# Index stage of a decoder layer: where the last query block's scratch lies and when scratch slots come back

## The chip, the cores and the metric

The kernel runs on one NeuronCore of a Trainium2 chip. The metric is the device time of one execution in microseconds (us). The engines have queues of their own, and each works through its queue in order: TensorE (PE, matmuls and transposes), VectorE (DVE), ScalarE (ACT), GpSimd (POOL, which also issues DMAs) and SyncE (SP, which issues most DMAs). [...]

## What is computed

The reference is one layer of a decoder: two attention mixers side by side (A: sparse attention with an indexer that selects keys; B: latent attention), gates, an output projection and a convolutional feed-forward part, on 512 tokens of width 2048, all in float32. The change lies in mixer A's indexer and in the projection behind it:

```python
dots = jnp.einsum('bthd,bsd->bths', qi_b, ki, preferred_element_type=jnp.float32)
score = jnp.einsum('bths,bth->bts', jax.nn.relu(dots), wi_b.astype(jnp.float32))
score = jnp.where(causal[None], score, -jnp.inf)
_, sel = lax.top_k(score, n_sel)
...
qa = apply_rope(rms_norm(qa.reshape(B, S, A_HEADS, A_HEAD_DIM), g_qa), *rope_a)
```

Each block of 128 queries has 16 index heads of width 64, and n_sel is 128. The first block needs no selection, since it sees at most 128 keys; blocks 1, 2 and 3 see 256, 384 and 512.

## The kernel before

**Buffers.** Storage that moves from use to use is a pool of slots of 128 x 512 numbers. `get()` takes a slot from the head of a list of free ones and `put()` gives one back to its end. Five wide buffers (`quad`, 128 x 2048) first form a ring `aring` through which the columns of w_ada pass; when that stage ends, four of them are taken out of the ring and cut into slots (`quad_views`), and the fifth, `aring[0]`, stays as a ring of one, for the rest of the w_ada stream that runs beside the attention stages. A framework puts a semaphore wait before every instruction that writes a slot which an earlier user still reads.

**Order.** The Python code issues instructions as a program would, and a scheduler then sets the order in each engine's queue by priorities and by a model of time. Which slot a step takes is settled in the Python order; when it may be written is then a matter of the chip.

**Weights.** Products run in three passes on a float32 that is split in a high and a low part. `wtile` loads a weight tile on SP, copies its high part on ACT (L145) and forms the low part on DVE (L146). The three matmuls of a product (`mm3`) stand on L157, L158 and L159. There are five raw buffers and three buffers of split tiles.

**Index stage.** The loop over query blocks `tb` 1 to 3 (L541) rotates the index queries of a block (`rope`, L505 to L508), transposes them (L549), splits them (L153, L154), and then, for each of 16 heads, multiplies with all keys up to S = 256, 384 or 512 (a dot of three matmuls), takes the relu on ACT (L563) into one of three slots `rl`, and adds it, weighted, to `acc` on DVE (L565, L567). The selection is DVE's alone: 16 maxima of eight (L575) with 15 replacements between them (L577) in `wk`, which is `rl[0]`, and then nine short steps (L582 to L591, the scan on L587 among them) that make the block's mask. At its end the four slots `acc`, `rl` are given back, in the Python order before the next block takes its own.

**First projections behind it.** `ev_qa` empties a bank of the query projection of mixer A: it takes a slot, copies the bank (L630), sums squares (L603, L604), normalises and rotates, transposes (L641) and writes the transposed rows (L643). The projection runs twice (`cb` 0 and 1), each time over eight weight tiles into banks 72 to 75 (`MM`), one for each block of tokens. Behind it come a product 320 wide (L793 to L803 empty and use it), one 512 wide, and the attention, whose first step that reads a mask is L684.

**Gate tiles.** Three tiles of the branch gates, computed with the first products into `part["B"][4:7]`, are stored to memory by POOL (L763), in the Python order only just ahead of the attention.

Of the kernel before, what the change touches and what calls it, by code (L numbers as in the profile page):

```python
# [10 lines left out]
F32 = mybir.dt.float32  # L11
# [7 lines left out]
P = 128  # L19
T = 512  # L20
D = 2048
KD = D // P
# [9 lines left out]
def trunk_layer_kernel(  # L32
# [19 lines left out]
    V, A, G, PE, SP = nc.vector, nc.scalar, nc.gpsimd, nc.tensor, nc.sync  # L52
# [4 lines left out]
    dram = ctx.enter_context(tc.tile_pool(name="scratch", bufs=1, space=bass.MemoryType.DRAM))  # L57
# [7 lines left out]
    def get(dt=F32, low=0):  # L65
        i = next((i for i in free if i >= low and (i < n_slots or dt == F32)), None)
        assert i is not None, (dt, list(free))
        free.remove(i)
        if i < n_slots and (cur[i] is None or cur[i].dtype != dt):
            cur[i] = pool.tile([P, T], dt, name=f"slot{i}", tag=f"slot{i}")  # L70
        held[id(cur[i])] = i
        return cur[i]
# [23 lines left out]
    def put(*ts):  # L96
        for t in ts:
            i = held.pop(id(t))
            if not isinstance(i, int):
                rfree.append(i)  # L100
            elif i not in retired:
                free.append(i)
# [53 lines left out]
    def mm3(o, lh, ll, rh, rl, first, last):  # L156
        PE.matmul(o, lh, rh, start=first, stop=False)  # L157
        PE.matmul(o, lh, rl, start=False, stop=False)  # L158
        PE.matmul(o, ll, rh, start=False, stop=last)  # L159
# [20 lines left out]
    def lin_tm(src, c0, n, act, K, banks, evac, k0=0, tick=None):  # L180
        for kg in range(0, K, 2):
            wh, wl = wtile(src, k0 + kg, 2, c0, n)
            for tb in range(4):
                ts = slice(tb * P, (tb + 1) * P)
                for i in range(2):
                    k = kg + i
                    ah, al = act[k]
                    mm3(banks[tb][:, :n], ah[:, ts], al[:, ts], wh[:, i, :], wl[:, i, :],
                        k == 0, k == K - 1)
                if kg + 2 == K:  # L190
                    evac(tb, banks[tb][:, :n])
            if tick:
                tick()
# [22 lines left out]
    aring = deque(quads[1:])  # L216
# [114 lines left out]
    part = {"A": [get() for _ in range(7)], "B": [get() for _ in range(7)]}  # L331
# [111 lines left out]
    f = 0  # L443
# [69 lines left out]
    def at_bank():  # L513
        cnt["at"] += 1
        return AT[cnt["at"] % 4]


    kit = part["A"][6]
    kw_tm = tslot[3][:, 0:320].rearrange("p (t n) -> p t n", t=4)
    kdup = tslot[4].rearrange("p (t a d) -> p t a d", t=4, a=2)  # L520
# [20 lines left out]
    for tb in range(1, 4):  # L541
        S = (tb + 1) * P
        qiT = []
        for cb in range(2):
            t = qi[tb, cb]
            rope(t.rearrange("p (h d) -> p h d", d=64), 8, 16, "i", tb)
            b = at_bank()
            for q in range(4):
                PE.transpose(b[:, q * P:(q + 1) * P], t[:, q * P:(q + 1) * P], ident)  # L549
            o = (getr(), getr())  # L550
            split(*o, b)
            put(t)
            qiT.append(o)
        acc = get()
        rl = [get(), get(), get()]
        for hd in range(16):
            ps = slice((hd % 2) * 64, (hd % 2) * 64 + 64)
            q = (hd % 8) // 2
            b = at_bank()
            (qh, ql), qs = qiT[hd // 8], slice(q * P, (q + 1) * P)  # L560
            mm3(b[:, :S], qh[ps, qs], ql[ps, qs], kiT[0][ps, :S], kiT[1][ps, :S], True, True)
            r = rl[hd % 3]
            A.activation(r[:, :S], b[:, :S], AF.Relu)  # L563
            if hd == 0:
                V.tensor_scalar(acc[:, :S], r[:, :S], wi[:, tb, 0:1], None, op0=ALU.mult)  # L565
            else:
                V.scalar_tensor_tensor(acc[:, :S], r[:, :S], wi[:, tb, hd:hd + 1], acc[:, :S],  # L567
                                       op0=ALU.mult, op1=ALU.add)
        put(*qiT[0], *qiT[1])
        V.tensor_tensor(acc[:, tb * P:S], acc[:, tb * P:S], Z[:, 384:512], ALU.add)  # L570
        m8 = sm.tile([P, 8], F32, name="m8")
        wk = rl[0]
        src = acc
        for it in range(16):
            V.max(m8, src[:, :S])  # L575
            if it < 15:
                V.match_replace(wk[:, :S], m8, src[:, :S], -3e38)  # L577
                src = wk
        thr = m8[:, 7:8]
        gt, eq, pre = rl[1][:, :S], rl[2][:, :S], wk[:, :S]  # L580
        cgt = sm.tile([P, 1], F32, name="cgt")
        V.tensor_scalar(gt, acc[:, :S], thr, None, op0=ALU.is_gt)  # L582
        V.tensor_reduce(cgt, gt, axis=AX.X, op=ALU.add)
        V.tensor_scalar(cgt, cgt, -1.0, 128.0, op0=ALU.mult, op1=ALU.add)
        V.tensor_scalar(eq, acc[:, :S], thr, None, op0=ALU.is_equal)
        V.memset(acc[:, :S], 1.0)
        V.tensor_tensor_scan(pre, acc[:, :S], eq, 0.0, ALU.mult, ALU.add)  # L587
        V.scalar_tensor_tensor(pre, pre, cgt, eq, op0=ALU.is_le, op1=ALU.mult)
        V.tensor_tensor(gt, gt, pre, ALU.add)
        mk = mask_at[tb].bitcast(BF)  # L590
        V.tensor_scalar(mk, gt, -NEG, NEG, op0=ALU.mult, op1=ALU.add)  # L591
        mask[tb] = mk
        put(acc, *rl)
    put(*kiT, tslot[3], tslot[4])
    mask[0] = Z[:, 384:512]

# [30 lines left out]
    def ev_qa(cb):  # L627
        def ev(tb, b):
            t = get()
            A.activation(t, b, AF.Copy)  # L630
            q3 = t.rearrange("p (n d) -> p n d", n=4)
            ss = sm.tile([P, 4], F32, name="ss4")
            head_ss(ss, q3, tb)
            n = nsc_a[:, tb, cb * 4:cb * 4 + 4]
            r = sm.tile([P, 4], F32, name="rs4")
            rsqrt_mean(r, ss, P, 4)
            V.tensor_scalar(n, r, -(P ** -0.5), None, op0=ALU.mult)
            rope(q3, 4, 32, "qa", tb)
            bb = at_bank()
            for q in range(4):  # L640
                PE.transpose(bb[:, q * P:(q + 1) * P], t[:, q * P:(q + 1) * P], ident)  # L641
            o = get()
            A.activation(o, bb, AF.Copy, scale=gq_col)  # L643
            put(t)
            qaT[tb, cb] = o
        return ev

    for cb in range(2):
        lin_tm(w_in, C_QA + cb * 512, 512, h, KD, MM, ev_qa(cb))


    att = {}
# [104 lines left out]
            pairs.append((th, tl))  # L757
        return pairs


    gate_d = [dram.tile([P, T], F32, name=f"gate{k}") for k in range(2 * KD)]
    for m in range(3):
        G.dma_start(gate_d[m], part["B"][4 + m])  # L763
        put(part["B"][4 + m])

    def ev_store(dst, j0):
        def ev(m, b):
# [259 lines left out]
    for i in range(KH // 2):  # L1027
        raw = [get() for _ in range(4)]
        ta, tb_ = get(), get()
        for j in range(2):  # L1030
            k, o = 2 * i + j, slice(j * HT, (j + 1) * HT)
# [692 lines left out]
    for q in range(NS):  # L1724
        p, k = q // NK, q % NK
# [89 lines left out]
```

## Time and profile before

| | |
|---|---|
| median of 3 runs | 2665.16 us (2662.46 to 2666.19) |
| the profiled execution | 2671.87 us |
| its span, first to last instruction | 2670.1 us |
| mean granted TensorE clock | 0.983 |
| index stage, second projection included | about 200 to 352 us of the span |

A row of the timeline reads: start in us, duration in us, engine, line, operation, written<-read, shape, count, and in brackets how long the engine was idle before it and what ended that. A row of the waits reads: who waited, for whom, us in total, times, longest. A row of a group reads: line, engine, operation, shapes, count | busy us, mean ns of one | idle us before it and what ended it. In the names of the trace the numbers are left out: `slot` is a single slot and `quad` a slot cut from a wide buffer.

### The profile page before, as it was taken

How to read it: one execution, taken by the hardware profiler on the slowest of the kernel's cores; microseconds unless marked ns; L12 is line 12 of the kernel's file. 1: busy time of each engine (PE TensorE's matmuls, PEld its weight loads, DVE VectorE, ACT ScalarE, POOL GpSimd, SP SyncE). 2: the span in 40 equal slices, each digit the busy share in tenths (PEclk: the TensorE clock that was granted, in tenths of full speed). 3: DMA queues.
4: the chain of work that ended last, by engine and by line, in shares of the span. 5: the costliest groups of instructions: out<-in, count | busy, mean ns of one | idle time of the engine just before them, and what ended most of it. 6: DMA issues, size and time to landing. Idle time of an engine off the chain costs nothing.

```text
span 2670.1 us, 39567 instructions
## 1 busy us (share of the span) xinstructions
PE 2576.3 (96%) x15210; PEld 2234.5 (84%) x15210; DVE 2109.8 (79%) x3130; ACT 1197.9 (45%) x1714; POOL 247.4 (9%) x483
## 2 busy tenths in 40 slices
PE   7999699998999999999999999999999999999988
PEld 5877487778997767888789999999999987877777
DVE  7968945768888666855679998998998987788876
ACT  5333333334445466322445555555555554443342
POOL 1000010000023132100000000000000000000000
PEclk8999799999999999999999999999999999999999
DMA  9932046663685488876224334434334357797776
GB/s 376 361 129 91 16 125 207 204 199 133 205 265 183 131 261 282 299 241 227 91 80 137 134 127 139 129 116 144 121 129 143 129 182 266 264 342 261 260 265 233
DMA packets 183044, 509.07 MB, mean 191 GB/s; under 512 B 20923, under 2 KB 29557, under 8 KB 182853
## 3 DMA queue, kind: packets, MB, share of 16 engines
q1 hardware_dynamic: 151460, 423.31, 47.2%
q0 software_dynamic: 31360, 83.21, 8.8%
q8 instruction: 119, 1.95, 0.3%
q14 instruction: 73, 0.59, 0.1%
q10 hardware_dynamic: 32, 0.01, 0.0%
HBM read 450.59 MB, written 55.85 MB: 190 GB/s over the span
## 4 chain that ended last, share of the span: by engine, by line
PE 81%; DVE 9%; DMA 7%; issue 1%; ACT 1%; SPq 0%; POOL 0%; DVEq 0%; ACTq 0%
PE bank L157 14%; PE bank L158 14%; PE bank L159 14%; PE bank L1015 11%; PE bank L1014 11%; PE bank L1016 11%; DMA wraw<-in_w_down 4%; DVE wsp L1462 2%; PE bank L703 1%; PE bank L1152 1%; PE bank L695 1%; PE bank L852 1%; DMA quad<-in_w_ada 1%; DVE wraw L1449 1%; DMA slot<-r 1%
## 5 line engine op out<-in xcount | busy, mean ns | idle before, releaser
L1015 PE MATMUL bank<-slot,wsp 128*128 128x256 f32 x2128 | 598.6, 281 | 0.4 <-DVE slot L154 0.4
L1014 PE MATMUL bank<-slot,wsp 128*128 128x256 f32 x2040 | 574.2, 281 | 3.7 <-ACT slot L153 2.5
L1016 PE MATMUL bank<-slot,wsp 128*128 128x256 f32 x2040 | 573.0, 281 | 0.0
L153 ACT ACTIVATE wsp<-wraw 128x1024 fp32r<-128x1024 f32 x336 | 356.5, 1061 | 449.4 <-PE bank L1015 340.6
L154 DVE TENSOR_TENSOR wsp<-wraw,wsp 128x1024 fp32r<-128x1024 f32 x336 | 410.2, 1222 | 76.8 <-ACT wsp L153 75.7
L158 PE MATMUL bank<-wsp,slot 128*128 128x512 f32 (+2 forms) x1108 | 437.0, 395 | 19.4 <-DVE wsp L1462 19.3
L159 PE MATMUL bank<-wsp,slot 128*128 128x512 f32 (+2 forms) x1166 | 450.2, 392 | 0.0
L157 PE MATMUL bank<-wsp,slot 128*128 128x512 f32 (+2 forms) x1108 | 394.3, 392 | 10.4 <-ACT wsp L1460 6.2
L1015 PEld LDWEIGHTS bank<-slot,wsp 128*128 128x128 f32 x2128 | 402.3, 189 | 0.7 <-DVE slot L154 0.6
L1014 PEld LDWEIGHTS bank<-slot,wsp 128*128 128x128 f32 x2040 | 385.7, 189 | 4.4 <-ACT slot L153 3.0
L1016 PEld LDWEIGHTS bank<-slot,wsp 128*128 128x128 f32 x2040 | 385.1, 189 | 0.0
L145 ACT ACTIVATE wsp<-wraw 128x1024 fp32r<-128x1024 f32 (+4 forms) x182 | 187.6, 1032 | 390.5 <-PE bank L159 190.8
L146 DVE TENSOR_TENSOR wsp<-wraw,wsp 128x1024 fp32r<-128x1024 f32 (+4 forms) x182 | 215.9, 1188 | 169.7 <-ACT wsp L145 169.2
L158 PEld LDWEIGHTS bank<-wsp,slot 128*128 128x128 f32 x1108 | 211.5, 191 | 71.2 <-DVE wsp L1462 25.4
L325 DVE CUSTOM_DVE_ANT_0 quad<-quad,quad,col 128x2048 f32<-128x2048 f32 x96 | 225.0, 2347 | 57.9 <-DMA quad<-in_w_ada 57.9
L159 PEld LDWEIGHTS bank<-wsp,slot 128*128 128x128 f32 x1166 | 222.4, 191 | 47.8 <-DVE slot L411 0.7
L157 PEld LDWEIGHTS bank<-wsp,slot 128*128 128x128 f32 x1108 | 209.9, 190 | 58.5 <-ACT wsp L1460 6.9
L907 DVE TENSOR_TENSOR wraw<-wraw 128x1024 f32<-128x1024 f32 x192 | 233.9, 1218 | 3.8 <-DMA wraw<-in_w_gs 2.0
L1460 ACT ACTIVATE wsp<-wraw 128x1536 fp32r<-128x1536 f32 (+1 forms) x109 | 151.5, 1397 | 154.1 <-DVE wraw L1452 80.7
L1462 DVE TENSOR_TENSOR wsp<-wraw,wsp 128x1536 fp32r<-128x1536 f32 (+1 forms) x109 | 179.0, 1645 | 29.2 <-ACT wsp L1460 29.2
L158 PE MATMUL bank<-slot,wsp 128*128 128x512 f32 (+1 forms) x414 | 166.2, 402 | 0.0
L157 PE MATMUL bank<-slot,wsp 128*128 128x512 f32 (+1 forms) x389 | 156.0, 405 | 0.0
(574 smaller groups left out, 4389.3 us busy)
## 6 DMA issues: line engine op xcount, KB each, us to landing
quad<-in_w_ada SPq DMA_DIRECT2D x192, 512.0 KB, 5.6
wraw<-in_w_ups SPq DMA_DIRECT2D x160, 512.0 KB, 3.4
wraw<-in_w_down SPq DMA_DIRECT2D x87, 768.0 KB, 5.8
wraw<-in_w_in SPq DMA_DIRECT2D x50, 512.0 KB, 3.5
wraw<-in_w_gs SPq DMA_DIRECT2D x32, 512.0 KB, 4.5
wraw<-in_w_o SPq DMA_DIRECT2D x32, 512.0 KB, 5.4
quad<-in_w_down SPq DMA_DIRECT2D x47, 256.0 KB, 4.5
wraw<-in_w_down SPq DMA_DIRECT2D x44, 256.0 KB, 5.4
```

The source lines that it names most:

```text
L146: w_ins[1] = V.tensor_tensor(lo, raw[:, :w], r32(hi), ALU.subtract)
L153: A.activation(dst_hi, src, AF.Copy)
L154: return V.tensor_tensor(dst_lo, src, r32(dst_hi), ALU.subtract)
L157: PE.matmul(o, lh, rh, start=first, stop=False)
L158: PE.matmul(o, lh, rl, start=False, stop=False)
L159: PE.matmul(o, ll, rh, start=False, stop=last)
L325: V.tensor_tensor_reduce(t, t, crow, 1.0, col1[:, j:j + 1], ALU.mult, ALU.add, mod[:, j:j + 1])
L907: V.tensor_tensor(o[:, :WN], a[:, :WN], b[:, :WN], op)
L1014: PE.matmul(o, wh[:, ks], rh, start=first and k == 0, stop=False, skip_group_check=True)
L1015: PE.matmul(o, wh[:, ks], rl, start=False, stop=False, skip_group_check=True)
L1016: PE.matmul(o, wl[:, ks], rh, start=False, stop=last, skip_group_check=True)
L1462: r = V.tensor_tensor(lo, t, r32(hi), ALU.subtract)
```

## The change

It does three things. The scratch of the third block that is worked on (`tb` 3) is no longer four slots but the four quarters of `aring[0]`. The scratch of `tb` 2 is kept in a list `busy` and given back only when both query projections have been issued; only that of `tb` 1 is given back in the loop. And the code that stores the three gate tiles, which gives their three slots back, moves ahead of the index stage.

```diff
+    gate_d = [dram.tile([P, T], F32, name=f"gate{k}") for k in range(2 * KD)]
+    for m in range(3):
+        G.dma_start(gate_d[m], part["B"][4 + m])
+        put(part["B"][4 + m])
+
     kit = part["A"][6]
...
-        acc = get()
-        rl = [get(), get(), get()]
+        if tb < 3:
+            acc, *rl = (get() for _ in range(4))
+        else:
+            acc, *rl = (aring[0][:, o:o + T] for o in range(0, 4 * T, T))
         for hd in range(16):
...
         mask[tb] = mk
-        put(acc, *rl)
+        if tb == 1:
+            put(acc, *rl)
+        elif tb == 2:
+            busy = [acc, *rl]
     put(*kiT, tslot[3], tslot[4])
...
     for cb in range(2):
         lin_tm(w_in, C_QA + cb * 512, 512, h, KD, MM, ev_qa(cb))
+    put(*busy)
...
-
-    gate_d = [dram.tile([P, T], F32, name=f"gate{k}") for k in range(2 * KD)]
-    for m in range(3):
-        G.dma_start(gate_d[m], part["B"][4 + m])
-        put(part["B"][4 + m])
```

The slots that later steps get change with it, and the scheduler orders the index stage and the projections anew. Line numbers behind the first insertion grow by 5, then by 7 and 10: L563, L567, L575, L577, L603, L630 and L641 of before are L570, L574, L582, L584, L613, L640 and L651 of the change.

On ACT, where the first query projection is emptied, before (`quad_70` is scratch of block 2, `slot_321` and `quad_71` of block 1, `slot_294` to `slot_298` of block 3; banks 72 to 75 hold the projection):

```order
L563 ACTIVATE slot_298<-bank_79 128x512
L630 ACTIVATE slot_321<-bank_72 128x512
L603 ACTIVATE slot_132<-slot_321 128x512
L563 ACTIVATE slot_294<-bank_76 128x512
L563 ACTIVATE slot_296<-bank_77 128x512
L603 ACTIVATE slot_132<-slot_325 128x512
L563 ACTIVATE slot_298<-bank_78 128x512
L630 ACTIVATE quad_71<-bank_73 128x512
```

And the last of the four, some ten rows further on in the same queue:

```order
L643 ACTIVATE slot_326<-bank_79,col_135 128x512
L643 ACTIVATE quad_71<-bank_78,col_135 128x512
L630 ACTIVATE quad_70<-bank_75 128x512
L603 ACTIVATE slot_329<-quad_70 128x512
L145 ACTIVATE wsp<-wraw 128x1024 x3
```

ACT's queue with the change, the same four steps (the relus around them are now those of block 2, 384 wide):

```order
L640 ACTIVATE slot_132<-bank_72 128x512
L613 ACTIVATE slot_133<-slot_132 128x512
L640 ACTIVATE slot_335<-bank_73 128x512
L613 ACTIVATE slot_294<-slot_335 128x512
L640 ACTIVATE slot_329<-bank_74 128x512
L613 ACTIVATE slot_133<-slot_329 128x512
L570 ACTIVATE quad_70<-bank_77 128x384
L570 ACTIVATE quad_70<-bank_78 128x384
L570 ACTIVATE quad_70<-bank_79 128x384
L145 ACTIVATE wsp<-wraw 128x1024
L640 ACTIVATE slot_324<-bank_75 128x512
```

The four copies now stand together, ahead of the dots of block 3, and none of their slots is scratch of a block.

On DVE, the weight splits (L146) around the end of block 2's selection, before (`m_1881` belongs to block 3):

```order
L591 TENSOR_SCALAR slot_316<-quad_70 128x384
L268 TENSOR_SCALAR rsm<-ss_2253 128x4
L577 MATCH_REPLACE slot_294<-m_1881,slot_294 128x512
L146 TENSOR_TENSOR wsp<-wraw,wsp 128x1024
L575 MAX m_1881<-slot_294 128x8
L637 TENSOR_SCALAR nsc_a<-rs_2256 128x4
L577 MATCH_REPLACE slot_294<-m_1881,slot_294 128x512
L146 TENSOR_TENSOR wsp<-wraw,wsp 128x1024
```

DVE with the change, the 15th split of the two projections (`quad_69` is the wide buffer, `quad_70` and `m_1773` belong to block 2):

```order
L574 SCALAR_TENSOR_TENSOR quad_69<-quad_69,wi 128x512
L584 MATCH_REPLACE quad_70<-m_1773,quad_70 128x384
L146 TENSOR_TENSOR wsp<-wraw,wsp 128x1024
L598 TENSOR_SCALAR wraw<-quad_71 128x256
L574 SCALAR_TENSOR_TENSOR quad_69<-quad_69,wi 128x512
L582 MAX m_1773<-quad_70 128x8
```

Before, no split stood between the 11th, early in block 2's sums, and the 12th, which is the first shown here, behind the mask of block 2 (L591). With the change the 11th to the 16th are spread over block 2's sums and selection and block 3's sums.

On PE, the second projection around the dots of block 3. Before, at the place where bank 75 is taken again (`wsp` are weights; `quad_70` is the first projection's fourth copy):

```order
L159 MATMUL bank_75<-wsp,slot_591 128x512
L641 MATMUL bank_76<-ident,quad_70 128x128 x4
L157 MATMUL bank_72<-wsp,slot_657 128x512
L157 MATMUL bank_73<-wsp,slot_657 128x512
L157 MATMUL bank_74<-wsp,slot_657 128x512
L157 MATMUL bank_75<-wsp,slot_657 128x512
```

PE with the change (rows from `quad_1359`, `quad_1360` are dots of block 3):

```order
L157 MATMUL bank_79<-quad_1359,quad_1360 128x512
L158 MATMUL bank_79<-quad_1359,quad_1360 128x512
L159 MATMUL bank_79<-quad_1359,quad_1360 128x512
L157 MATMUL bank_73<-wsp,slot_798 128x512
L158 MATMUL bank_73<-wsp,slot_798 128x512
L159 MATMUL bank_73<-wsp,slot_799 128x512
L157 MATMUL bank_76<-quad_1359,quad_1360 128x512
L158 MATMUL bank_76<-quad_1359,quad_1360 128x512
L159 MATMUL bank_76<-quad_1359,quad_1360 128x512
L157 MATMUL bank_74<-wsp,slot_754 128x512
```

Before, the first three tiles of the second projection ran bank by bank, with bank 75 last and all dots of block 3 ahead of it; now its matmuls and the dots alternate. Ahead of 200 us and from the attention on, all five queues hold the same instructions in the same order as before, but for one matmul that changes places on PE much later.

## The prediction

> **What bounds the kernel now.** I read the page first, for where TensorE (PE) is not busy; then busy time by stretch; then the waits; then the timeline of ACT and PE.
>
> ```profile
> span 2670.1 us, 39567 instructions
> PE   7999699998999999999999999999999999999988
> PEclk8999799999999999999999999999999999999999
> PE 81%; DVE 9%; DMA 7%; issue 1%; ACT 1%; SPq 0%; POOL 0%; DVEq 0%; ACTq 0%
> ```
>
> PE carries the chain that ended last. After the start the only weak slice is the fifth (267 to 334 us), with six tenths of PE and seven of its clock: the index stage. By stretch:
>
> ```profile
> 257.90:272.00 14.10, 13.60 (x73) 9.77 (x73) 13.75 (x38) 7.66 (x15) 0.00 (x0) 1.00 0.12 38
> 272.00:296.30 24.30, 22.53 (x84) 15.28 (x82) 24.30 (x70) 11.96 (x21) 3.46 (x3) 0.79 0.00 0
> 296.30:317.00 20.70, 0.00 (x0) 0.00 (x0) 20.67 (x56) 1.59 (x3) 0.00 (x0) 0.59 0.00 0
> 317.00:351.60 34.60, 34.57 (x145) 28.07 (x146) 27.95 (x64) 11.89 (x16) 2.55 (x3) 0.95 0.24 68
> 351.60:381.20 29.60, 29.60 (x207) 29.57 (x206) 10.88 (x29) 12.42 (x25) 3.48 (x5) 1.00 0.38 118
> ```
>
> The columns are the stretch and its length, then busy us (and instructions) of PE, weight load, DVE, ACT, POOL, then PE's clock and DMA. PE does nothing for 20.7 us from 296.3. DVE is full from 272 to 317, and half empty again from 351.6.
>
> ```profile
> PE bank L157 <- ACT quad L630: 20.7, 1, 20.7
> ACT quad L630 <- DVE quad L587: 19.1, 1, 19.1
> 256.00 0.62 ACT L630 ACTIVATE slot<-bank 128x512 f32<-128x512 f32 x1
> 279.68 0.60 ACT L630 ACTIVATE slot<-bank 128x512 f32<-128x512 f32 x1
> 285.65 0.59 ACT L630 ACTIVATE quad<-bank 128x512 f32<-128x512 f32 x1
> 316.38 0.60 ACT L630 ACTIVATE quad<-bank 128x512 f32<-128x512 f32 x1 [19.09 <-DVE quad L587]
> 317.03 0.80 PE L157 MATMUL bank<-wsp 128*128 128x512 f32 x1 [20.75 <-ACT quad L630]
> ```
>
> L630 empties a bank of the first query projection into a slot. Of its four calls the third has a free slot and runs at 256.00. The first two take scratch of query block 1 and wait for its selection (279.68, 285.65). The last takes `quad_70`, scratch of query block 2, whose selection reads it last in the scan of L587, so it runs at 316.38. Bank 75 stays full until then, and PE's queue has the second projection's matmuls on that bank next. So what ends last is a slot, not arithmetic.
>
> **The change part by part.** No instruction is added or removed on any engine; the order differs only between about 200 and 440 us.
>
> *The stall.* PE's own work in the stretch is counted from its queue, at these paces:
>
> ```profile
> 254.67 0.34 PE L157 MATMUL bank<-quad,quad 64*128 64x384 f32 x1
> 254.85 0.34 PE L158 MATMUL bank<-quad,quad 64*128 64x384 f32 x1
> 257.48 0.39 PE L158 MATMUL bank<-wsp,slot 128*128 128x512 f32 x1
> 257.71 0.40 PE L159 MATMUL bank<-wsp,slot 128*128 128x512 f32 x1
> 273.31 0.49 PE L157 MATMUL bank<-quad,quad 64*128 64x512 f32 x1 [0.55 <-ACT slot L563]
> 282.75 0.63 PE L157 MATMUL bank<-wsp 128*128 128x512 f32 x1
> 283.18 0.63 PE L158 MATMUL bank<-wsp 128*128 128x512 f32 x1
> ```
>
> From start to start a 512-wide matmul takes 0.23 us (257.48 to 257.71; 0.231 over longer runs) and a 384-wide one 0.175; at the lowered clock the 512 takes 0.43. The first projection's last matmul ends at 257.9 and the first 320-wide matmul of the next product starts at 351.6: 93.7 us. Between them stand 192 matmuls of the second projection and 48 dots of query block 3 (240 x 0.231 = 55.4), 24 dots of block 2 (4.2) and 32 transposes at about 0.09 (2.9): **62.5 us of work, 31.2 us lost**. Of the loss 20.7 is the stall, 1.8 the nine matmuls at 0.43 instead of 0.23 just after it, and 8.7 the small waits and lowered clock between 268 and 296, where PE has little but block 3's dots and each waits for ACT and DVE. In the new order these dots stand among the second projection's matmuls.
>
> *What is late next: the splits.* Each 1024-wide weight tile needs one split on DVE (L146). Now six of the sixteen (the 11th to the 16th) stand among the selection steps of blocks 1 and 2 and the sums of block 3. DVE's prices:
>
> ```profile
> L146 DVE TENSOR_TENSOR wsp<-wraw,wsp 128x1024 fp32r<-128x1024 f32 x11 | 13.4, 1215 | 4.5 <-ACT wsp L145 4.5
> L567 DVE SCALAR_TENSOR_TENSOR slot<-slot,wi,slot 128x512 f32<-128x512 f32 x15 | 11.0, 732 | 0.0
> L567 DVE SCALAR_TENSOR_TENSOR quad<-quad,wi 128x384 f32<-128x384 f32 x15 | 9.1, 606 | 0.4 <-ACT quad L563 0.4
> L575 DVE MAX8 m<-quad 128x8 f32<-128x384 f32 x16 | 8.6, 537 | 0.0
> L577 DVE MATCH_REPLACE8 quad<-m,quad 128x384 f32<-128x384 f32 x15 | 8.0, 531 | 0.0
> L575 DVE MAX8 m<-slot 128x8 f32<-128x256 f32 x16 | 6.8, 422 | 0.1
> L577 DVE MATCH_REPLACE8 slot<-m,slot 128x256 f32<-128x256 f32 x15 | 6.1, 409 | 0.0
> L567 DVE SCALAR_TENSOR_TENSOR slot<-quad,wi,slot 128x256 f32<-128x256 f32 x10 | 4.8, 484 | 4.4 <-ACT quad L563 3.9
> L567 DVE SCALAR_TENSOR_TENSOR slot<-slot,wi,slot 128x256 f32<-128x256 f32 x5 | 2.4, 485 | 1.0 <-ACT slot L563 0.7
> 249.86 1.23 DVE L146 TENSOR_TENSOR wsp<-wraw,wsp 128x1024 fp32r<-128x1024 f32 x1 [0.51 <-ACT wsp L145]
> 297.47 0.67 DVE L575 MAX8 m<-slot 128x8 f32<-128x512 f32 x1
> 298.07 0.53 DVE L575 MAX8 m<-quad 128x8 f32<-128x384 f32 x1
> ```
>
> Mean ns of one stands behind the busy time. The tenth split starts at 249.86; with the six short rows after it DVE comes to the first rope of the emptied projection near 254. From there to the 16th split its queue holds 6 splits (7.3), 14 sums of 512 (10.2) and 13 of 384 (7.9), 9 maxima (4.8) and 9 replacements (5.4, with a value load of 0.07) of 384, 11 and 11 of 256 (4.6 and 5.3), and 41 others, 13.2 by the same view: 58.7 us of durations. Neighbours overlap by 0.06 to 0.07 (297.47 + 0.67 against 298.07), 8 us over 134 instructions, so about 50.5. The 16th split is done between 304.5 and 312.7. PE without waits comes to its tile at 257.9 + 62.5 - 5.5 = 314.9. **The splits are in time, by 2 to 10 us.**
>
> The next product (eight narrow tiles, 29.6 us on PE, row 351.60) brings the end of block 2's selection and most of block 3's: 41.0 us of durations, 35 overlapped, to the last narrow split. That is 340 to 354; PE wants it at 257.9 + 62.5 + 29.6 - 3.7 = 346.3. From 6 early to 7.4 late: a loss of 0 to 7.4, taken at 1. Here alone the cover is thin. Small waits (the first dots behind their splits, transposes behind ropes) I put at 2 more.
>
> *The wide buffer.* Sums from wide and from single slots cost the same (484 and 485 ns above), so the move itself costs 0. But `quad_69` is the ring of the w_ada stream. Its first load, and what else rests on the selection:
>
> ```profile
> 391.78 0.97 SPq L320 DMA_DIRECT2D quad<-in_w_ada  x2
> 339.64 0.43 DVE L591 TENSOR_SCALAR slot<-slot 128x512 bf16<-128x512 f32 x1
> 443.52 0.75 DVE L684 CUSTOM_DVE_ANT_0 slot<-bank,slot,nsc_a 128x512 f32<-128x512 f32 x1
> 201.79 0.62 POOL L763 DMA_DIRECT2D gate<-slot  x1 [182.17 <-DVE rsm L268]
> ```
>
> The load would move from 391.8 to about 361. Block 3's mask, done by 340 before, now stands behind the fourth split of the product after the narrow one, also near 360: the load may wait 0 to 2 us, and the weight loads behind it on SP's queue with it. They run ahead into five buffers; I take 0. The mask is first read by L684, at 443.5 - 31 = 412, 50 us later. So deferring block 3 is covered.
>
> *Held slots and gate stores.* The three stores already ran at 201.79 and in the two us after; they keep their place on POOL's queue: 0. One of their slots, the key tile's, one of block 1 and a free one now take the first projection, so all four banks empty by about 259. Block 2's slots come back after both projections, before anyone asks for them.
>
> **Sum:** 31.2 less 3 = 28 us. The profiled execution took 2671.9 (span 2670.1), so 2643.9 of its kind; the three runs have a median of 2665.2, 6.7 lower, and I predict against that: **2637**. Behind 440 us the queues are as before, but for one matmul, and PE sets the pace, so the gain stays.
>
> **Rivals.**
>
> *DVE becomes the bound.* The last narrow split comes 7.4 late, and block 3's dots cost PE the 8.7 us they cost before although other matmuls stand between: 16 us of the 31 go, 2649 (2643 to 2655). For it: DVE is full and in order, and every relu, rope and split must pass it. Against it: the overlapped sum leaves PE 6 to 10 us.
>
> *The wait only moves.* Another bank finds its slot busy, and the change does not do what it says: about 2664. For it: before, two more of the four calls had waited on a selection (279.68, 285.65). Against it: the four new holders are given up before 259, and none is selection scratch.
>
> *Slower.* PE, fed by DVE in small portions, drops to the low clock and stays there. The row at 282.75 shows this clock after waits of 0.55 us (273.31 and its neighbours). Price: 0.43/0.23 puts 0.86 us on each us of work, 54 on all 62.5, less 31.2: 2688. It decides from 36 of the 62.5 us at the low clock; before, some 14 us ran so (clock 0.79 over 24.3 us and 0.95 over 34.6, in the rows by stretch, if the low clock is half). Against it: a late split makes PE wait once and then run on, and the clock was back after 10 us.
> [...]
>
> **How the numbers follow.** Forecast 0.66 (2632 to 2643), DVE bound 0.24, wait only moved 0.06, slower 0.04. What a measurement can tell from no change is 0.2%, 5.3 us: faster 0.90, same 0.06, slower 0.04. The range runs from 2630 (all 31.2, and runs that spread by 2 to 3 us) to 2655, the end of the second case, and leaves out the last two.
>
> **What would show it.** Right: the four evacuations of the first projection run between 252 and 260 with no wait on DVE; no PE gap over 2 us between 258 and 350; the first 320-wide matmul near 321 to 324 instead of 351.6; L684 some 28 us earlier; all later stages shifted by the same amount. If DVE binds, PE or ACT waits for L146, or for the sums at each dot, and the lowered clock shows. If the wait moved, one gap of 10 us or more stands at another evacuation. Wrong altogether would be a shift at 351.6 that is lost again by 600.

## The result

| | before | with the change |
|---|---|---|
| first comparison: median (lowest to highest), four executions each | 2663.81 us (2662.40 to 2666.19) | 2640.76 us (2635.68 to 2642.41) |
| ratio of the times | | 0.9896, 95% interval 0.9877 to 0.9915 |
| second comparison, later, beside the experiments: median | 2670.16 us | 2637.97 us (2635.52 to 2641.73) |
| ratio | | 0.9881, interval 0.9866 to 0.9896 |
| profiled execution (span) | 2671.87 us (2670.1) | 2642.41 us (2640.6) |

The forecast was 2637. The page of the changed kernel, the lines that answer to those shown of before: its span, PE's busy share and granted clock in 40 slices, and the shares of the chain that ended last.

```profile
span 2640.6 us, 39567 instructions
PE   7999999998999999999999999999999999999988
PEclk8999999999999999999999999999999999999999
PE 84%; DMA 7%; DVE 6%; issue 1%; ACT 1%; SPq 0%; DVEq 0%; ACTq 0%
```

The weak fifth slice is gone from both lines, and DVE's share of the chain has fallen. By stretch, after (the stretch and its length, then busy us and instructions of PE, weight load, DVE, ACT and POOL, then PE's clock and DMA):

```profile
258.00:272.00 14.00, 14.00 (x61) 9.52 (x60) 14.00 (x45) 5.83 (x11) 4.86 (x3) 1.00 0.21 62
272.00:300.00 28.00, 28.00 (x119) 17.88 (x117) 26.32 (x64) 11.87 (x19) 0.00 (x0) 1.00 0.13 36
300.00:326.00 26.00, 26.00 (x126) 20.59 (x126) 22.92 (x56) 13.37 (x21) 0.98 (x1) 1.00 0.14 39
326.00:360.00 34.00, 34.00 (x223) 32.93 (x223) 32.33 (x93) 14.06 (x33) 6.08 (x8) 1.00 0.42 134
```

In these stretches PE is busy in every microsecond and its clock is never lowered. DVE was as full before; now PE is full beside it. The timeline of the first projection's four evacuations on ACT, and of PE where the 320-wide product begins, first of the change, then of before:

```profile
251.93 0.59 ACT L640 ACTIVATE slot<-bank 128x512 f32<-128x512 f32 x1
253.10 0.58 ACT L640 ACTIVATE slot<-bank 128x512 f32<-128x512 f32 x1
254.25 0.58 ACT L640 ACTIVATE slot<-bank 128x512 f32<-128x512 f32 x1
257.88 0.58 ACT L640 ACTIVATE slot<-bank 128x512 f32<-128x512 f32 x1
324.50 0.30 PE L157 MATMUL bank<-wsp 128*128 128x320 f32 x1
```

```profile
351.19 0.30 PE L157 MATMUL bank<-wsp 128*128 128x320 f32 x1
```

No evacuation waits for DVE any more: the last runs at 257.88 instead of 316.38. (The start of the 320-wide product in before is 351.19; the prediction had read 351.6 from the edge of a stretch.)

**A common zero.** Executions differ by up to 5 us in the start-up (the row below starts between 189.96 and 194.81 in the profiles of all kernels here), so places in two traces are compared from a row that stands ahead of everything that the change moves: ACT's copy of a 1024-wide weight tile, near 191 us. Of before, and of the change:

```profile
191.17 1.06 ACT L145 ACTIVATE wsp<-wraw 128x1024 fp32r<-128x1024 f32 x1 [3.92 <-PE bank L158]
```

```profile
190.86 1.06 ACT L145 ACTIVATE wsp<-wraw 128x1024 fp32r<-128x1024 f32 x1 [3.92 <-PE bank L158]
```

From there the 320-wide product begins after 160.0 us before and 133.6 after, 26.4 earlier. The large product near 600 us shows what is left of that. Its summary by line gives counts, durations and the first and last start, of before (L1014) and of the change (L1020):

```profile
L1014 PE MATMUL bank<-wsp x184: 276/281/385, 618.2 to 2193.7; 128*128 128x256 f32 x184
```

```profile
L1020 PE MATMUL bank<-wsp x184: 276/281/385, 591.4 to 2165.2; 128*128 128x256 f32 x184
```

It begins 427.0 us behind the common row before and 400.5 after: 26.5. So the gain arises between 258 and 325 us and stays. These two distances carry most of what follows, since they repeat: two profiles of the change gave 133.6 and 400.5 both times, while their spans differ by 5.3 us (2640.6 and 2635.3), all of it behind 2165. The times follow them only to some us: from its first matmul to its last the large product takes 1575.5 to 1581.6 us in the profiles of all kernels here, and what lies behind it 467 to 477.

### The profile page after: what moved, and what is told of

Same layout as the page of the kernel before. It is cut to its first block, busy times and chain, and to the rows that moved or that the text cites. A ratio compares the mean times of both kernels' runs of the same rounds, so it can differ in the third digit from the quotient of the medians.

```text
span 2640.6 us, 39567 instructions
## 1 busy us (share of the span) xinstructions
PE 2570.7 (97%) x15210; PEld 2225.4 (84%) x15210; DVE 2108.6 (80%) x3130; ACT 1198.3 (45%) x1714; POOL 249.7 (9%) x483
## 4 chain that ended last, share of the span: by engine, by line
PE 84%; DMA 7%; DVE 6%; issue 1%; ACT 1%; SPq 0%; DVEq 0%; ACTq 0%
PE bank L157 15%; PE bank L158 15%; PE bank L159 15%; PE bank L1020 11%; PE bank L1021 11%; PE bank L1022 11%; DMA wraw<-in_w_down 3%; DVE wsp L1468 2%; PE bank L714 1%; PE bank L1158 1%; DMA slot<-r 1%; PE bank L706 1%; PE bank L858 1%; DVE wraw L1455 1%; DMA wraw<-in_w_in 1%
## 5 line engine op out<-in xcount | busy, mean ns | idle before, releaser
L1020 PE MATMUL bank<-slot,wsp 128*128 128x256 f32 x2040 | 573.4, 281 | 3.6 <-ACT slot L153 2.4
L1020 PEld LDWEIGHTS bank<-slot,wsp 128*128 128x128 f32 x2040 | 384.3, 188 | 4.3 <-ACT slot L153 2.9
L146 DVE TENSOR_TENSOR wsp<-wraw,wsp 128x1024 fp32r<-128x1024 f32 (+4 forms) x182 | 215.5, 1187 | 141.8 <-ACT wsp L145 140.9
```

Of the source, the lines that this page charges most:

```text
L146: w_ins[1] = V.tensor_tensor(lo, raw[:, :w], r32(hi), ALU.subtract)
L1020: PE.matmul(o, wh[:, ks], rh, start=first and k == 0, stop=False, skip_group_check=True)
```

## The experiments

The theory, **S**: the slot that each of the four evacuations takes sets the time. Before, the last one took scratch of block 2; any change that keeps the four off that scratch removes the stall, and the gain depends on whether some of them still take scratch of block 1. Its rivals: that the parts of the change add up, each with its own share (A), or that DVE is the bound of this stretch (B and D).

All results in one table; the distances are from the common row to the 320-wide product and to the product near 600.

| kernel | median, us | before beside it | ratio, 95% interval | to 320 | to 600 |
|---|---|---|---|---|---|
| before | | | | 160.0 | 427.0 |
| the change | 2640.76; 2637.97 | 2663.81; 2670.16 | 0.9896 (0.9877 to 0.9915); 0.9881 (0.9866 to 0.9896) | 133.6; 133.6 | 400.5; 400.5 |
| gate stores alone | 2654.11 | 2668.24 | 0.9944 (0.9924 to 0.9964) | 139.0 | 405.9 |
| block 2 held alone | 2661.37 | 2668.24 | 0.9982 (0.9968 to 0.9996) | 131.9 | 417.4 |
| wide buffer alone | 2651.42 | 2668.24 | 0.9929 (0.9906 to 0.9953) | 136.9 | 403.9 |
| wide buffer, gate stores | 2644.98 | 2668.24 | 0.9916 (0.9895 to 0.9938) | 133.6 | 404.7 |
| wide buffer, held | 2645.65 | 2670.16 | 0.9908 (0.9894 to 0.9923) | 135.8 | 402.8 |
| gate stores, blocks 2 and 3 held | 2651.68 | 2671.47 | 0.9924 (0.9896 to 0.9952) | 139.0 | 405.9 |
| the change, fourth copy in block 2's slot | 2672.80 | 2670.16 | 1.0014 (1.0004 to 1.0024) | 160.3 | 427.2 |
| the change, 16 steps more on DVE | 2642.56 | 2671.47 | 0.9892 (0.9866 to 0.9918) | 134.8 | 401.7 |
| the change, 48 steps more on DVE | 2644.14 | 2671.47 | 0.9898 (0.9874 to 0.9922) | 132.2 | 404.2 |
| the change, dots of 128 rows | 2641.64; 2640.70 | 2670.16; 2671.47 | 0.9900 (0.9882 to 0.9917); 0.9885 (0.9858 to 0.9912) | 130.6; 130.6 | 397.5; 397.6 |

### The change again

> The whole change again, to narrow its interval and to stand beside the three others on the same chip. 2636 to 2645 us, 20 to 28 us less than the kernel before on this chip; first 320-wide matmul about 27 us earlier than before.

2637.97 us; the 320-wide product 26.4 us earlier from the common row, as in the first profile.

### One slot put back

```diff
-            t = get()
+            t = busy.pop() if (cb, tb) == (0, 3) else get()
```

> The whole change, but the fourth copy of the first query projection is made to take a slot of block 2's scratch again (the held list gives it), as before the change. Wide buffer, early gate stores and the rest stay. Theory S (the slot of that copy is the cause of the 20.7 us stall): PE stalls at bank 75 until block 2's selection has read its scores, 10 us or more in one piece, and the time is 2652 to 2664 us. Rival (the wide buffer and the new order by themselves bring it, and the slot only went along): 2638 to 2645 us, no gap over 2 us.

The timeline of this kernel, ACT's fourth evacuation and PE's next matmul on that bank:

```profile
315.63 0.60 ACT L640 ACTIVATE quad<-bank 128x512 f32<-128x512 f32 x1 [17.02 <-DVE quad L595]
316.28 0.80 PE L157 MATMUL bank<-wsp 128*128 128x512 f32 x1 [18.39 <-ACT quad L640]
```

One slot gives the whole gain back: 18.4 us of stall in one piece, again behind the selection of block 2, and 160.3 and 427.2 us on the table, those of before. The time (2672.80) lies above the range given. The wide buffer, the early stores and three held slots are all still there. The edit is not a pure one: with that slot the scheduler, which models the wait, also puts the fourth evacuation some 30 rows later in ACT's queue, and the rows of PE and DVE around it with it. Slot and order go together here, and the trace shows only that the wait on the selection is what ends last. That the slot is enough without that order is not shown by this kernel; the three below, which take the last copy off block 2's scratch in three other ways, all lose the stall.

### Each part alone

Each is the kernel before with one hunk of the diff. Of gate stores alone:

```diff
+    for m in range(3):
+        G.dma_start(gate_d[m], part["B"][4 + m])
+        put(part["B"][4 + m])
+
     kit = part["A"][6]
```

> The kernel before with the early gate stores alone: the scratch of block 3 is in single slots again and all scratch is given back in the loop, so of the change only the two or three slots that come back earlier are left. The first query projection is then emptied into two free slots and into two slots of block 1's scratch, and none of its four copies takes a slot of block 2. Theory S (what counts is the slot that each of the four copies takes): the stall of 20.7 us at bank 75 goes though neither the wide buffer nor the held slots are there; two copies still wait for block 1's selection, which ends near 280 us, so some of the 8.7 us of small waits stay. Expected 2641 to 2650 us, against 2664 before and 2641 with the whole change. Rival A (the wide buffer and the held slots bring the time, the gate stores only fit in): 2659 to 2664. Rival B (DVE is close to the bound, and only the spread of the splits saved it): the stall turns up at another bank, 2655 to 2664, with PE waiting for L146.

Of block 2 held alone:

```diff
-        put(acc, *rl)
+        if tb == 2:
+            busy = [acc, *rl]
+        else:
+            put(acc, *rl)
...
+    put(*busy)
```

> The kernel before with the held scratch of block 2 alone. Two of the four copies of the first projection take free slots, two take slots of block 1's scratch, none a slot of block 2. Theory S: as with the gate stores alone, 2641 to 2650 us. Rival A1 (the parts add up, and the held slots are the smaller part beside the wide buffer): 2655 to 2664. Rival A2 (the held slots are the change, the two others only keep the pool from running dry): 2641, and the gate stores alone and the wide buffer alone at 2659 or more.

Of the wide buffer alone:

```diff
+        if tb < 3:
+            acc, *rl = (get() for _ in range(4))
+        else:
+            acc, *rl = (aring[0][:, o:o + T] for o in range(0, 4 * T, T))
...
-        put(acc, *rl)
+        if tb < 3:
+            put(acc, *rl)
```

> The kernel before with the wide buffer for block 3 alone. Two of the four copies take free slots, two take slots of block 1's scratch. Theory S: as the two others, 2641 to 2650 us; the sum of the three single gains is then two to three times the gain of the whole change. Rival A (parts add up): the three single gains add to the 23 us of the whole, so this one gives at most what the other two leave.

In all three the four evacuations are over by 294 us and the 20.7 us stall at bank 75 is gone, with 21.0, 28.1 and 23.1 us gained at the 320-wide product. The parts do not add up: at 600 us they are worth 21.1, 9.6 and 23.1, together 53.8, against 26.5 for all. That is against rival A. The times of the gate stores (2654.11) and of the wide buffer (2651.42) lie 4 and 1 us above my range all the same, and that of the held slots misses it by 11. The 2661.37 of the held slots lies in the range of rival A1, though for a reason that A1 did not name, the second one below. Some of the difference lies in the comparison, in which the kernel before took 2668 and not the 2664 of which the ranges were made. The rest has two reasons.

The first is what is left where two evacuations take scratch of block 1. PE's timeline with the gate stores alone, dots of block 3:

```profile
278.91 0.50 PE L157 MATMUL bank<-quad,quad 64*128 64x512 f32 x1 [0.56 <-ACT slot L567]
280.43 0.49 PE L157 MATMUL bank<-quad,quad 64*128 64x512 f32 x1 [0.56 <-ACT slot L567]
281.94 0.49 PE L157 MATMUL bank<-quad,quad 64*128 64x512 f32 x1 [0.56 <-ACT slot L567]
283.59 0.79 PE L157 MATMUL bank<-quad,quad 64*128 64x512 f32 x1 [0.56 <-ACT slot L567]
284.18 0.62 PE L158 MATMUL bank<-quad,quad 64*128 64x512 f32 x1
284.61 0.62 PE L159 MATMUL bank<-quad,quad 64*128 64x512 f32 x1
```

While two banks of the projection stay full, PE has only dots to do, each held by a relu, and at 283.6 its clock drops: from start to start a matmul then takes 0.43 us (284.18 to 284.61) instead of 0.23. The granted clock between 272 and 300 is 0.82 there and 1.00 with the whole change. This costs 5.4 us at the 320-wide product (139.0 against 133.6), and 3.3 with the wide buffer alone.

The second is specific to the held slots. They remove block 2's slots from the second projection too, one of whose copies then gets scratch of block 3, on ACT and PE:

```profile
344.06 0.60 ACT L632 ACTIVATE slot<-bank 128x512 f32<-128x512 f32 x1 [19.69 <-DVE slot L586]
344.70 0.63 PE L157 MATMUL bank<-wsp 128*128 128x320 f32 x1 [16.32 <-ACT slot L632]
```

PE has by then begun the narrow product (at 322.94) and stops in it for 16.3 us. Alone, the held slots move the wait, as the second rival of the prediction had it for the whole change.

### Two parts of three

The change without the held slots, without the early gate stores, and without the wide buffer (there block 3's scratch, single slots again, is held with block 2's):

```diff
-        elif tb == 2:
-            busy = [acc, *rl]
```

> The change without the held scratch: wide buffer and early gate stores. The four copies of the first projection take the same four free slots as with the whole change; the last copy of the second projection takes a slot of block 2. Theory S: 2638 to 2645 us, the same as the whole change within 3 us, since block 2's selection has long ended when the second projection is emptied. Rival A2 (the held slots carry the gain): 2655 or more, with a wait at the second projection's last copy.

```diff
-    for m in range(3):
-        G.dma_start(gate_d[m], part["B"][4 + m])
-        put(part["B"][4 + m])
-
     kit = part["A"][6]
```

> The whole change without the early gate stores: wide buffer and held slots. The first projection's copies take two free slots and two of block 1's scratch, as with the wide buffer alone. Theory S: 2647 to 2655 us, as with the wide buffer alone (2651), since the same four slots are taken; the gate stores are worth 8 to 10 us, which is the wait for block 1's selection. Rival (the wide buffer and the held slots carry all, gate stores only fit in): 2638 to 2645 us.

```diff
-        if tb < 3:
-            acc, *rl = (get() for _ in range(4))
-        else:
-            acc, *rl = (aring[0][:, o:o + T] for o in range(0, 4 * T, T))
+        acc, *rl = (get() for _ in range(4))
...
+        else:
+            busy += [acc, *rl]
```

> Early gate stores, and the scratch of blocks 2 and 3 held until both query projections are issued, with single slots for block 3 instead of the wide buffer. The first projection takes two free slots and two of block 1's scratch; the second takes none of block 3's. Theory S (the wide buffer is worth what its four slots are worth as holders, and nothing by itself): no gap at a copy of the second projection, where holding block 2 alone had one of 16 us; 2644 to 2653 us, as with the other kernels whose first projection takes two slots of block 1. Rival (a scratch in the wide buffer is what makes block 3 fast): 2658 or more.

Wide buffer and gate stores have the same four slots as the whole change and reach the 320-wide product after the same 133.6 us; but the last copy of the second projection to run (339.54) waits for block 2's selection, which the expectation had put at nothing. PE waits 2.2 us for it, its clock is lowered for a moment behind that (0.95 granted between 326 and 360, 1.00 with the whole change), and 4.2 us are lost by 600. This is what the held slots are worth in the whole change. Wide buffer and held slots have two slots of block 1 and lose 2.2 us at the first place and 2.3 at the second. The time, 2645.65, falls between my range for S and the rival's: I had put the early stores at 8 to 10 us there, by the distances about four times too much. The medians differ by 7.7 (2645.65 against 2637.97); what this has beyond the distances is not explained. With both blocks held in single slots the 16 us gap at the second projection is gone, and the two distances are 139.0 and 405.9, those of the gate stores alone, whose four slots it shares. So the wide buffer is worth what its four slots are worth as places to put things.

### How much cover DVE has

```diff
             A.activation(r[:, :S], b[:, :S], AF.Relu)
+            for _ in range(1 if tb == 3 else 0):
+                V.tensor_scalar(r[:, :S], r[:, :S], 1.0, None, op0=ALU.mult)
```

> The whole change with 16 more DVE steps: each score tile of block 3 is multiplied in place by 1 before it is added (128x512, some 0.47 us by the rows of that form, 7.5 us in all). In the change the 16th split is done at 308 us, where PE comes to its tile at 319, and the last narrow split starts at 344, wanted at 350. Theory C (DVE has cover, 11 us for the second projection and 6 for the narrow product): 0 to 2 us longer than the whole change, 2636 to 2643 us, no PE gap over 2 us before 324. Rival D (DVE is the bound of this stretch, since it is busy 0.93 of it): all 7.5 us show, 2645 to 2650.

With three such steps in place of one:

> The same with 48 more steps, 22.6 us of DVE. The scheduler knows of them and puts some dots of block 3 later on PE, so that sums move into the time from 360 us on, where DVE was busy 12 of 30 us. Theory C: the cover is used up but the rest goes into that idle time; 2 to 10 us longer than the whole change, 2640 to 2650, with PE waiting for DVE or for relus between 300 and 390. Rival D: 20 us longer or more, 2658 to 2665.

By their own rows the 16 steps took 6.7 us (0.42 each, where 0.47 was expected) and the 48 took 20.0. At 600 us the 6.7 show as 1.2 and the 20.0 as 3.7; the medians are 2642.56 and 2644.14, within the ranges of theory C. PE has no gap in either, where theory C had expected waits for the larger dose. The 1.2 need not be DVE's: the scheduler's new order has PE go to the dots 28 times up to the 320-wide product, where the change has 27, and lets fewer of their matmuls run side by side (39 against 42). At the prices of the next section that comes to about 1 us. Where the larger dose went, in the stretches of that kernel:

```profile
326.00:360.00 34.00, 34.00 (x232) 33.16 (x231) 31.57 (x89) 17.77 (x40) 4.95 (x5) 1.00 0.41 119
360.00:390.00 30.00, 30.00 (x135) 24.26 (x134) 27.14 (x63) 6.46 (x7) 2.81 (x6) 1.00 0.47 139
```

From 360 to 390 DVE is busy 27.14 us, where the change itself has 12.12. The scheduler had put sums of block 3 there. A full DVE is therefore not yet a bound here: most of its work has no one waiting. Both doses were free to be reordered, so this holds for the scheduler's orders and not for one fixed order.

### What the remaining microseconds are

PE without a wait took 66.6 us from 257.9 to 324.5, where the prediction had counted 62.5. Five of the counted matmuls, 1.2 us, now run before 257.9, so the count for this stretch is 61.3 and 5.3 are missing. PE's timeline with the change, where it goes to the dots and comes back, and the weight loads (PEld) beside them:

```profile
262.06 0.39 PE L159 MATMUL bank<-wsp 128*128 128x512 f32 x1
262.29 0.39 PE L157 MATMUL bank<-wsp 128*128 128x512 f32 x1
262.61 0.44 PE L157 MATMUL bank<-quad 64*128 64x384 f32 x1
262.89 0.33 PE L158 MATMUL bank<-quad 64*128 64x384 f32 x1
263.06 0.34 PE L159 MATMUL bank<-quad 64*128 64x384 f32 x1
263.33 0.50 PE L158 MATMUL bank<-wsp 128*128 128x512 f32 x1
263.66 0.39 PE L159 MATMUL bank<-wsp 128*128 128x512 f32 x1
262.61 0.18 PEld L157 LDWEIGHTS bank<-quad 64*128 64x128 f32 x1 [0.36 <-issue]
```

The last matmul of 128 rows ahead of the dots takes 0.32 us from start to start (262.29 to 262.61) where its neighbours take 0.23, and the last dot 0.27 (263.06 to 263.33) where the one before it takes 0.17. The rows behind the changes are longer too: the first dot takes 0.28 (262.61 to 262.89) and the first matmul of 128 rows 0.33 (263.33 to 263.66). That is 0.09 and 0.11 on the way in and 0.09 and 0.10 on the way back, 0.39 us for a visit to the dots. The weights of the first dot are loaded only at 262.61, when its matmul begins.

The new order itself raises the number of visits. Before, PE goes to the dots 6 times between 257.9 and 351.2; with the change, whose dots stand among the projection's matmuls, 18 times. Something is given back where two dots stand together, since neighbouring heads use different halves of the 128 rows. An x2 stands for two matmuls that start within 0.01 us of each other:

```profile
285.30 0.50 PE L157 MATMUL bank<-quad,quad 64*128 64x512 f32 x2
285.63 0.40 PE L158 MATMUL bank<-quad,quad 64*128 64x512 f32 x2
285.87 0.40 PE L159 MATMUL bank<-quad,quad 64*128 64x512 f32 x2
286.10 0.39 PE L157 MATMUL bank<-quad,quad 64*128 64x512 f32 x1
```

Six matmuls take the time of three here (0.80 us from 285.30 to 286.10, with the 0.10 of the first dot). The test has dots of 128 rows, half of them zeros; it takes one slot more, and block 1's scratch is held too, so that the four evacuations keep free slots:

```diff
+    for d, kd in enumerate((kdup, kdup2)):
+        V.memset(kd[:, :, 1 - d, :], 0.0)
+        V.tensor_copy(kd[:, :, d, :], kw_tm[:, :, 0:64])
...
-            mm3(b[:, :S], qh[ps, qs], ql[ps, qs], kiT[0][ps, :S], kiT[1][ps, :S], True, True)
+            kh, kl = kih[hd % 2]
+            mm3(b[:, :S], qh[:, qs], ql[:, qs], kh[:, :S], kl[:, :S], True, True)
```

> The whole change, with index dots of 128 rows instead of 64: the key tile exists twice, each time with the rows of the other head set to zero, so that a dot multiplies all 128 rows of a query tile; the result is the same. It adds four transposes, one split and two memsets, about 3 us of DVE ahead of block 1, and holds block 1's scratch as well so that the four copies of the first projection still take free slots. Theory R (PE loses about 0.1 us at each change between matmuls of 128 and of 64 rows and again behind it, 18 visits to the dots in the stretch from 258 to 324 us and as many before): the first 320-wide matmul comes 3 to 6 us earlier and the time is 2635 to 2639 us where the whole change has 2641. Rival R2 (the change of weights, bank or shape costs it, whatever the rows): the same time within 1.5 us. Rival R3 (the added DVE work shows, since DVE is busy 0.93 of this stretch): 2642 to 2646 us.

> The kernel with 128-row dots again, for more runs: its first profile had the first 320-wide matmul 3.0 us nearer to a common early row than the whole change has, and 3.0 us less where the next stage starts, but its four times had a median of 2641.6 against 2638.0. Theory R: the 3 us are real and the tail of the program scatters by more than that; the median of all runs is 2635 to 2640 us. Rival R3: something later pays them back, the median stays at 2640 to 2644, and the rows behind 600 us show where.

PE's timeline and a weight load of this kernel at such a place:

```profile
261.75 0.39 PE L159 MATMUL bank<-wsp 128*128 128x512 f32 x1
261.99 0.34 PE L157 MATMUL bank<-quad,quad 128*128 128x384 f32 x1
262.17 0.35 PE L158 MATMUL bank<-quad,quad 128*128 128x384 f32 x1
263.40 0.34 PE L159 MATMUL bank<-quad,quad 128*128 128x384 f32 x1
263.58 0.39 PE L159 MATMUL bank<-wsp,slot 128*128 128x512 f32 x1
263.81 0.40 PE L157 MATMUL bank<-wsp,slot 128*128 128x512 f32 x1
261.76 0.19 PEld L157 LDWEIGHTS bank<-quad,quad 128*128 128x128 f32 x1
```

The changes cost nothing now (0.24 and 0.18 ahead of them, 0.18 and 0.23 behind), no two dots run side by side any more, and the weights of the dot that starts at 261.99 are loaded at 261.76, under the matmul before. At the 320-wide product and at 600 us the kernel is 3.0 us ahead of the change, in both profiles. So far theory R holds, against R2 and R3. The 3.0 is what is left of more: up to the 320-wide product the change makes 27 visits, an estimated 10.5 us at 0.39, and has 42 matmuls beside another, 6.8 us at their paces; the test loses both and has four transposes more (0.4), 3.3 us less in all. The times don't show it, and by them alone R2 and R3 would stand: eight executions have a median of 2640.7 (2636.4 to 2646.8), the eight of the change 2639.3 (2635.5 to 2642.4). Nothing behind 600 us was found that pays the 3 us back: the last matmul of the product near 600 is still 3 us ahead in both profiles (1973.0 and 1974.0 us behind the common row, against 1976.1 and 1977.2). What lies behind it takes between 467 and 474 us in two profiles of the change, and 469 and 473 here. Whether the 3 us are lost in the scatter or paid for in executions that have no profile stays open. It is no better version by the times.

## Why the prediction was right

**The stall.** The cause is shown, not only argued: putting the one slot back, with the order that the scheduler then chose, restores 18.4 us of stall and all of the time, and three kernels that take the copy off that slot in other ways have no such stall. The four evacuations run between 251.9 and 258.5 without a wait, as foretold, and PE is busy without a gap up to 390. The 320-wide product starts at 324.5, just behind the 321 to 324 that were named.

**The count of PE's work** was too small by 5.3 us (61.3 for what stands in the stretch, 66.6 taken). Paces were read inside runs of one shape, and the changes between 128 and 64 rows were put at nothing, though the new order triples them. The 18 visits to the dots come to 7.0 us at 0.39 each, the 12 matmuls of this stretch that run beside another take 2.5 off, and the transposes with the matmuls around them add 0.7: 5.2. That is an account from one trace; the test with 128 rows bears out its first two terms together, 3.0 us measured where they and the transposes gave 3.3.

**The losses that I allowed for** (1 for the narrow product, 2 for small waits) did not occur. That the two errors nearly cancel is luck: the sum said 28 us, the traces have 26.5.

**The small waits and the lowered clock** (8.7 us before) were rightly named as removable, but not all of the 8.7 is theirs. It was what the count left over, and of the 26.4 us gained at the 320-wide product 20.7 are the stall and 1.8 the slow matmuls behind it, so 3.9 came from here, net of the visits that the new order adds. The kernels with two slots of block 1 keep 2.2 to 5.4 us of them, so what removes them is that all four slots are free, and for that the wide buffer and the early stores are needed together.

**The splits.** The 16th was to end between 304.5 and 312.7 and the last narrow one between 340 and 354. DVE's timeline:

```profile
306.51 1.23 DVE L146 TENSOR_TENSOR wsp<-wraw,wsp 128x1024 fp32r<-128x1024 f32 x1 [1.86 <-ACT wsp L145]
344.43 0.82 DVE L146 TENSOR_TENSOR wsp<-wraw,wsp 128x640 fp32r<-128x640 f32 x1 [0.69 <-ACT wsp L145]
```

Both lie inside. The narrow product, called the thin place, had more cover than I gave it, because PE came to it 4 us later than in the count without waits (324.5 against 257.9 + 62.5): the 16 steps more on DVE cost 1.2.

**The wide buffer and block 3's late mask.** The load of w_ada was put at 361 and the mask near 360. They came at 365.9 and 366.6, and PE stayed busy throughout, so the 0 that I took holds.

**The rivals.** DVE as the bound is refuted by the two doses. The wait that only moves is real, 16.3 us with the held slots alone and 2.2 us in the change without them, but not in the change itself. The slow clock has a place too: with the gate stores alone it comes where PE is fed dots one by one, for some 10 us (an estimate from 0.82 over 28 us and from 0.50, the granted clock of before between 278 and 286, where matmuls of 512 took the same 0.43), and the whole change has no such stretch.

**The basis.** The forecast took 28 from a median of 2665.2. The medians beside the change were 2663.8 and 2670.2, and differences of medians 23 and 32 us stand on both sides of the 26.5 that the traces show at 600 us. 26.5 of 2665 is a ratio of 0.990, inside the first interval and just above the end of the second (0.9896). What the second comparison has beyond 26.5 is not explained.

## What to carry to other kernels

When a pool hands out slots in program order, look at who last reads the slot of each step that empties a matmul bank: one copy into the scratch of a long, unfinished chain can stop TensorE until that chain has read it (20.7 and 18.4 us here), and the busy shares show that TensorE stands still but not for what. Several unrelated edits to the pool can each remove such a wait, so their single gains must not be added, and an edit that only withholds slots may hand the wait to the next step that asks. Before an engine that is 90% busy is called the bound, load it further and see whether anyone waits.

## What the hardware showed that I had not expected

In the change, going from matmuls of 128 rows to matmuls of 64 rows and back lengthens the matmul ahead of each step and the one behind it, by 0.09 and about 0.10 us (0.32 and 0.33 against 0.23, 0.27 and 0.28 against 0.17). The next weights aren't loaded ahead at these places: at the visit shown they are loaded at 262.61 and 263.33, when their own matmuls start. With 128 rows throughout they are (at 261.76 for the dot of 261.99), and the cost is gone (0.24 and 0.18, 0.18 and 0.23); so is the gain of dots that run two at a time in the two halves of the rows (six in 0.80 us).

PE's clock fell without any long wait. In the kernel with the gate stores alone a matmul takes 0.43 us from start to start instead of 0.23 from 283.6 on, after five microseconds of dots with idle pieces of 0.56 us in each 1.5 us, the longest that PE had from 250 on. With the wide buffer alone the granted clock between 272 and 300 is 0.82 as well, behind the same waits (0.54 to 0.56 us), and in the kernel before it was 0.50 between 278 and 286, behind waits of 0.55 and 0.56. In these three kernels no idle piece longer than 0.56 us stood ahead of the low clock from 250 on.
